# Alternating reads of the streamed operand, and one 512-column product per high part, in a hybrid decoder layer

## The chip, the cores and the metric

The kernel runs on one core of a Trainium2 chip. The metric is the time of one execution on the device in microseconds (us); of several runs the median is given. The core has a matrix engine (TensorE, in the profile PE, its weight loads PEld), a vector engine (DVE), a scalar engine (ACT), GpSimd (POOL) and SyncE (SP), which issues most of the DMAs.

## What is computed

The reference is one decoder layer for 256 positions and a model width of 2048, in float32. Cut to what matters:

```python
h = rmsnorm(x, attn_norm_w)
z, xbc, dt_raw, q, k, v, g = split(h @ w_in)          # 2048 -> 4096, 6144, 64, 3 x 2048, 4096
y_ssm  = ssd_mixer(z, xbc, dt_raw, ...) @ w_ssm_out   # 4096 -> 2048
y_attn = moba_attention(q, k, v, ...) @ w_attn_out    # 2048 -> 2048
g_ssm, g_attn = split(sigmoid(g + b_gate))
x = x + (g_ssm * y_ssm + g_attn * y_attn) @ w_out
h = rmsnorm(x, ffn_norm_w)
u_gate, u_up = split(causal_dwconv(h @ w_up, ...))    # 2048 -> 2 x 5632
x = x + (silu(u_gate) * u_up) @ w_down                # 5632 -> 2048
```

With 256 positions, attention has one block, and the SSD mixer one chunk.

## The kernel before

Nearly all the work is large products of a weight matrix with the 256 positions. A product in float32 is made of three products in a shorter float form (F32R): each operand is split into a high part (a rounded copy) and a low part (what is left), and high x high, high x low and low x high are summed.

**A unit.** The weights come in units of 128 partitions x 2048 columns, that is 16 blocks of 128 x 128: 128 output channels, all 2048 input channels. `unit` (L172) issues the unit's DMA (1 MB, on SP) into `wraw`, and splits it in two chunks of 1024 columns: ACT copies the high part `whi` (L182), DVE subtracts to get the low part `wlo` (L183). `wraw`, `whi` and `wlo` have three buffers each, so `whi` and `wlo` hold a unit and a half.

**Its products.** `cm_unit` (L220) lets `cm_chunk` (L211) run through the blocks of each chunk: for every block of the high part two matmuls of 256 columns with the same weights, one streaming the inputs' high part `xh` (L215), one the low part `xl` (L216); then for every block of the low part one matmul with `xh` (L218). The weights are the stationary operand, the 256 positions the streamed one. So a unit has 48 matmuls, all of them accumulated in 256 columns of one PSUM bank (tile `mm`, four buffers). Each matmul loads its own weights.

**Inputs.** `r32` (L240) makes tiles with both parts of an input, 2 x 16 x 256 columns: `hp` (the input with the norm's weights, for value, query, key and attention-gate units), `ot` (attention), `hn` (the normed input, for the SSD and SSD-gate units), `yt` (SSD output, 2 x 8 blocks), `mt` (the merged branches), `fh` (the second norm's input), and `a0`, `a1` (activations of the up products, in three parts of 16, 16 and 12 blocks). They share three slots.

**Order.** First the value products: here the inputs are stationary and the weights streamed, 512 columns at a time (`tm_chunk`, L370; L376, L377 and L382 are high x high, low x high and high x low). Then eight attention pairs of four query and key units each (L574), the last value block among them; attention's small work is spread over them step by step (`Spread`), and a hand-written order of PE holds in this stage. Then 16 gate units (`gate_attn`, L610) and 16 attention output units (L670); then, with the order left to the scheduler, eight SSD groups of ten units (L747) with the SSD core's steps between them, among these the product `ydot` (L834), whose streamed operand `mhl` holds a high and a low part (L840: 2 x 256 columns, L841: 2 x 128); 16 SSD gate units (L900) and 32 SSD output units (`out_unit`, L882); 16 output units (`out_products`, L966); and 88 up units (`up`, L999) and 48 down units (`down`, L1027) in thirds.

**What takes a product away.** Each unit's sum in PSUM is read by ACT or DVE: query and key units by ACT (square and scaled copy, L451 and L452), gates by DVE (L614), attention output by DVE (L672), SSD units by ACT and three DVE products (L753 to L757), output units by DVE (L976, then ACT L977 and DVE L978 write `fh`), up units by DVE (L1013, then ACT L1015 and DVE L1018 do the convolution), down units by DVE (L1038). The last down unit is added in two halves of 128 columns (L1035), each sent out by its own DMA.

Of the kernel before, what the change touches and what calls it, by code (L numbers as in the profile page):

```python
# [8 lines left out]
F32 = mybir.dt.float32  # L9
# [112 lines left out]

# [38 lines left out]
def _body(tc, nc, d, out):  # L161
# [48 lines left out]

    def cm_chunk(ps, part, xh, xl, k0, nk, first, last):  # L211
        hi, lo = part
        for k in range(nk):
            w = hi[:, k * 128:(k + 1) * 128]
            PE.matmul(ps, w, xh[:, k0 + k], start=first and k == 0, stop=False)  # L215
            PE.matmul(ps, w, xl[:, k0 + k], start=False, stop=False)  # L216
        for k in range(nk):
            PE.matmul(ps, lo[:, k * 128:(k + 1) * 128], xh[:, k0 + k], start=False, stop=last and k == nk - 1)  # L218

    def cm_unit(src, xh, xl, nk=16):  # L220
        parts = unit(src, nk * 128)
        ps = mm_tile()[:, :T]
        for c in range(2):
            cm_chunk(ps, parts[c], xh, xl, c * nk // 2, nk // 2, c == 0, c == 1)
        return ps
# [17 lines left out]

    _, hph, hpl = r32("hp")
    xt_full = xs_slot("xt")
# [124 lines left out]
    def tm_chunk(pst, part, k0, first, last):  # L370
        hi, lo = part
        for k in range(2):
            wh = hi[:, k * 512:(k + 1) * 512]
            for tt in range(2):
                ts = slice(tt * 128, (tt + 1) * 128)
                PE.matmul(pst[tt], hph[:, k0 + k, ts], wh, start=first and k == 0, stop=False)  # L376
                PE.matmul(pst[tt], hpl[:, k0 + k, ts], wh, start=False, stop=False)  # L377
        for k in range(2):
            wl = lo[:, k * 512:(k + 1) * 512]
            for tt in range(2):  # L380
                ts = slice(tt * 128, (tt + 1) * 128)
                PE.matmul(pst[tt], hph[:, k0 + k, ts], wl, start=False, stop=last and k == 1)  # L382

# [51 lines left out]

    _, oh_, ol_ = r32("ot")
    ap.tile([128, 8], F32, name="pad3")
# [6 lines left out]
    def attn_pair(j):  # L444
        st = {}

        def evac(key, h, ps):
            if h == 0:
                st["n" + key] = ap.tile([128, 2, T], F32, name="n" + key, bufs=2)
                st["s" + key] = ap.tile([128, 2, T], F32, name="sq", bufs=2)  # L450
            S.activation(st["s" + key][:, h], ps, AF.Square)  # L451
            S.activation(st["n" + key][:, h], ps, AF.Copy, scale=sm("qn") if key == "q" else kscale)  # L452

# [118 lines left out]
        for i in range(4):  # L572
            key = "qk"[i // 2]
            evac(key, i % 2, cm_unit(d["wqk"][j, i], hph, hpl))  # L574
# [55 lines left out]
    sp.tick()  # L630
    pg6 = cm_unit(d["wga"][6], hph, hpl)
    sp.flush()
# [7 lines left out]
    def hn_steps():  # L640
        xr = {}

        def load(c):
            def f():
                xr[c] = xb.tile([128, 4, T], F32, name="xr", bufs=2)
                nc.gpsimd.dma_start(xr[c], d["xT"][:, 4 * c:4 * c + 4])
            return f

        def norm(c):
            def f():  # L650
                x = xr.pop(c)
# [3 lines left out]
                S.activation(hnh[:, ks], x, AF.Copy)  # L655
                V.tensor_tensor(hnl[:, ks], x, hnh[:, ks].bitcast(F32), op=SUB)
            return f

        return [[load(0), load(1)], [], [norm(0), load(2)], [], [norm(1), load(3)], [], norm(2), [], norm(3)]

    sp.add(hn_steps(), 18)
    for o in range(KT):
# [5 lines left out]
        if o == 3:  # L668
            gl[6] = gate_attn(6, pg6)
        po = cm_unit(d["wao"][o], oh_, ol_)  # L670
        g = gl.pop(o)
        V.tensor_tensor(g, g, po, op=MUL)  # L672
        if o % 2:
# [21 lines left out]
    def dt_unit():  # L695
# [4 lines left out]
        for c in range(2):  # L700
# [4 lines left out]
            for k in range(8):  # L705
                wk = w[:, k].rearrange("p a c -> p (a c)")
                PE.matmul(ps, wk, hnh[:, 8 * c + k], start=c == 0 and k == 0, stop=False)
                PE.matmul(ps, wk, hnl[:, 8 * c + k], start=False, stop=c == 1 and k == 7)
        return ps
# [34 lines left out]
    def group_units(g):  # L744
        pr = pre[g % 2]
        for i in range(10):
            ps = cm_unit(d["wssd"][g, i], hnh, hnl)  # L747
            if i < 4:
# [11 lines left out]
    def core_steps(g):  # L760
# [73 lines left out]
        def ydot(p):  # L834
            def f():
                m = st.pop(("m", p))
                for h in range(2):
                    ps = c_tile().rearrange("p (a t) -> p a t", t=T)
                    x0, x1 = [st["x"][:, s, p, 2 * h:2 * h + 2].rearrange("p a c -> p (a c)") for s in range(2)]
                    PE.matmul(ps, x0, m[:, :, h, 0:256], start=True, stop=False)  # L840
                    PE.matmul(ps[:, :, 128:], x1, m[:, :, h, 256:384], start=False, stop=True)  # L841
                    rs, ls = slice(h * 64, (h + 1) * 64), slice(64 - h * 64, 128 - h * 64)
# [39 lines left out]
    def out_unit(q, u, done):  # L882
        parts = unit(d["wso"][q, u])
        yh, yl = yt[:, q % 2, 0], yt[:, q % 2, 1]
        ps = mm_tile()
        for c in range(2):
            cm_chunk(ps[:, c * T:(c + 1) * T], parts[c], yh, yl, 0, 8, True, True)
        done(u, ps.rearrange("p (a t) -> p a t", t=T))

    def acc_done(q):  # L890
        def f(u, ps):
            y = yacc[:, 2 * u:2 * u + 2]
            if q == 0:
# [5 lines left out]
    def gate_ssm(o):  # L899
        pg = cm_unit(d["wgs"][o], hnh, hnl)  # L900
        if o >= 8:
# [30 lines left out]

    _, mh_, ml_ = r32("mt")

    def merge(u, ps):
# [10 lines left out]
        nc.gpsimd.dma_start(a, ma[u])  # L946
        V.tensor_tensor(yacc[:, os_], ps, yacc[:, os_], op=ADD)
        V.tensor_tensor(yacc[:, os_], yacc[:, os_], g, op=MUL)
# [12 lines left out]
    for c in range(4):  # L961
        S.dma_start(x1[:, 4 * c:4 * c + 4], d["xT"][:, 4 * c:4 * c + 4])
    _, fh, fl = r32("fh")
    ssum = fp.tile([128, T], F32, name="ssum")

    def out_products():  # L966
        parts = [unit(d["wout"][o]) for o in range(2)]
        pss = [mm_tile()[:, :T] for _ in range(2)]
        for c in range(2):
            for o in range(2):  # L970
                cm_chunk(pss[o], parts[o][c], mh_, ml_, 8 * c, 8, c == 0, c == 1)
        for o in range(KT):
# [26 lines left out]
    def up(th):  # L999
# [5 lines left out]
        for i in range(n):  # L1005
            cv = []
            for half in range(2):
                ti = half * NFF + f0 + i
                ps = cm_unit(d["wup"][ti], fh, fl)
# [3 lines left out]
                V.tensor_tensor(u, ps, fr, op=MUL)  # L1013
                c = fp.tile([128, T], F32, name=f"c{half}", bufs=2)
# [12 lines left out]
    def down(th):  # L1027
        at = acts[th]
        n = thirds[th][1]
        for o in range(KT):  # L1030
            ps = cm_unit(d[wd[th]][o], at[:, 0], at[:, 1], n)
            if th == 2 and o == KT - 1:
                for h, q in enumerate((S, nc.sync)):
                    hs = slice(h * 128, (h + 1) * 128)
                    V.tensor_tensor(x1[:, o, hs], ps[:, hs], x1[:, o, hs], op=ADD)  # L1035
# [35 lines left out]
```

## Time and profile before

| | |
|---|---|
| median of 3 runs | 2019.43 us |
| lowest and highest | 2018.99, 2019.73 us |
| span of the profiled execution, first to last instruction | 2017.6 us |
| instructions in the span | 40769 |
| from HBM, to HBM | 394.44 MB, 5.33 MB |
| DMA issues of 1 MB | one per unit, landing some 4.8 us after issue |

The profiled execution's own time is known by its span alone; it lies 1.8 us under the median of the runs. The profile's lines give for a group of instructions the line of the kernel, the engine, what is written and read, the shape and the number; behind the bar the busy time in us, the mean duration of one in ns, and the idle time of the engine before them with what ended it. [...] The timeline gives start and duration of instructions in us.

### The profile page before, as it was taken

To read this page: it belongs to the slowest core of one execution; us is meant where nothing else is said; L and a number is where in the kernel's file an instruction comes from. 1 tells how busy PE (TensorE), PEld (TensorE's weight loads), DVE (VectorE), ACT (ScalarE), POOL (GpSimd) and SP (SyncE) were. 2 spreads that over 40 slices of the span, in tenths; PEclk is the share of its full clock that TensorE was granted. 3 is DMA by queue.
4 is the path that set the end of the run, shared out by engine and by line. 5 is a ranking of instruction groups with operands and counts; after the bars stand their busy time and mean duration, and the time that the engine had idled before them with its cause. 6 is when DMAs were issued, how large, how long until landed. Compare 5 with 4: busy or idle time off the path is not lost.

```text
span 2017.6 us, 40769 instructions
## 1 busy us (share of the span) xinstructions
PE 2012.3 (100%) x17203; PEld 1989.1 (99%) x17203; DVE 1496.5 (74%) x2214; ACT 1189.5 (59%) x1640; POOL 79.0 (4%) x100
## 2 busy tenths in 40 slices
PE   9999999999999999999999999999999999999999
PEld 7999999999999999999999999999999999999999
DVE  7588877656788798888989886677777765677554
ACT  6466655544768867667677645565555553455333
POOL 0012210000000000000000000000000000000000
PEclk9999999999999999999999999999999999999999
DMA  7555555656556555555565575555555555555555
GB/s 290 188 187 183 181 177 206 234 204 215 188 192 217 205 199 208 194 196 190 196 208 178 197 276 200 190 189 198 199 189 191 201 194 189 194 201 190 190 186 169
DMA packets 64351, 402.40 MB, mean 199 GB/s; under 512 B 7655, under 2 KB 10264, under 8 KB 20648
## 3 DMA queue, kind: packets, MB, share of 16 engines
q1 hardware_dynamic: 55384, 376.56, 52.9%
q0 software_dynamic: 5760, 18.97, 3.1%
q10 hardware_dynamic: 3024, 4.27, 0.6%
q8 instruction: 134, 2.20, 0.4%
q14 instruction: 49, 0.40, 0.1%
HBM read 394.44 MB, written 5.33 MB: 198 GB/s over the span
## 4 chain that ended last, share of the span: by engine, by line
PE 99%; DVE 0%; DMA 0%; issue 0%; SPq 0%; ACT 0%; DVEq 0%
PE mm L215 31%; PE mm L218 31%; PE mm L216 31%; PE mm L382 1%; PE mm L376 1%; PE mm L377 1%; PE cc L840 1%; PE cc L841 0%; PE cc L793 0%; DMA wraw<-wv 0%; PE cc L228 0%; PE cc L229 0%; PE cc L230 0%; PE cc L561 0%; DVE wlo L183 0%; DVE xt L318 0%
## 5 line engine op out<-in xcount | busy, mean ns | idle before, releaser
L182 ACT ACTIVATE whi<-wraw 128x1024 fp32r<-128x1024 f32 (+1 forms) x712 | 744.7, 1050 | 664.7 <-PE mm L216 583.2
L183 DVE TENSOR_TENSOR wlo<-wraw,whi 128x1024 fp32r<-128x1024 f32 (+1 forms) x712 | 864.1, 1218 | 242.9 <-ACT whi L182 238.0
L215 PE MATMUL mm<-hn,whi 128*128 128x256 f32 x1536 | 358.7, 277 | 0.0
L216 PE MATMUL mm<-hn,whi 128*128 128x256 f32 x1536 | 358.3, 277 | 0.0
L215 PE MATMUL mm<-fh,whi 128*128 128x256 f32 x1408 | 327.9, 277 | 0.0
L216 PE MATMUL mm<-fh,whi 128*128 128x256 f32 x1408 | 327.8, 276 | 0.0
L215 PEld LDWEIGHTS mm<-hn,whi 128*128 128x128 f32 x1536 | 288.4, 188 | 1.5 <-ACT whi L182 0.2
L216 PEld LDWEIGHTS mm<-hn,whi 128*128 128x128 f32 x1536 | 288.5, 188 | 0.1
L215 PEld LDWEIGHTS mm<-fh,whi 128*128 128x128 f32 x1408 | 264.4, 188 | 0.0
L216 PEld LDWEIGHTS mm<-fh,whi 128*128 128x128 f32 x1408 | 264.3, 188 | 0.0
L218 PE MATMUL mm<-hn,wlo 128*128 128x256 f32 x1536 | 205.6, 277 | 0.0
L218 PEld LDWEIGHTS mm<-hn,wlo 128*128 128x128 f32 x1536 | 188.4, 188 | 0.0
L218 PE MATMUL mm<-fh,wlo 128*128 128x256 f32 x1408 | 188.2, 277 | 0.0
L215 PE MATMUL mm<-hp,whi 128*128 128x256 f32 x768 | 180.1, 278 | 0.0
L216 PE MATMUL mm<-hp,whi 128*128 128x256 f32 x768 | 179.2, 277 | 0.0
L218 PEld LDWEIGHTS mm<-fh,wlo 128*128 128x128 f32 x1408 | 172.7, 188 | 0.0
L215 PE MATMUL mm<-a,whi 128*128 128x256 f32 x704 | 164.4, 277 | 0.0
L216 PE MATMUL mm<-a,whi 128*128 128x256 f32 x704 | 164.3, 276 | 0.0
L216 PEld LDWEIGHTS mm<-hp,whi 128*128 128x128 f32 x768 | 144.3, 188 | 0.1
L215 PEld LDWEIGHTS mm<-hp,whi 128*128 128x128 f32 x768 | 144.3, 188 | 0.1
L215 PEld LDWEIGHTS mm<-a,whi 128*128 128x128 f32 x704 | 132.2, 188 | 0.0
L216 PEld LDWEIGHTS mm<-a,whi 128*128 128x128 f32 x704 | 132.2, 188 | 0.0
(308 smaller groups left out, 3244.1 us busy)
## 6 DMA issues: line engine op xcount, KB each, us to landing
wraw<-wup SPq DMA_DIRECT2D x88, 1024.0 KB, 4.8
wraw<-wssd SPq DMA_DIRECT2D x80, 1024.0 KB, 4.9
wraw<-wqk SPq DMA_DIRECT2D x32, 1024.0 KB, 4.8
wraw<-wso SPq DMA_DIRECT2D x32, 1024.0 KB, 4.9
wraw<-wd SPq DMA_DIRECT2D x32, 1024.0 KB, 4.8
wraw<-wga SPq DMA_DIRECT2D x16, 1024.0 KB, 5.0
wraw<-wao SPq DMA_DIRECT2D x16, 1024.0 KB, 5.0
wraw<-wgs SPq DMA_DIRECT2D x16, 1024.0 KB, 4.8
```

What stands on the lines that cost most here:

```text
L182: last_hi[0] = S.activation(hi[:, :n // 2], raw[:, s], AF.Copy)
L183: V.tensor_tensor(lo[:, :n // 2], raw[:, s], hi[:, :n // 2].bitcast(F32), op=SUB)
L215: PE.matmul(ps, w, xh[:, k0 + k], start=first and k == 0, stop=False)
L216: PE.matmul(ps, w, xl[:, k0 + k], start=False, stop=False)
L218: PE.matmul(ps, lo[:, k * 128:(k + 1) * 128], xh[:, k0 + k], start=False, stop=last and k == nk - 1)
L376: PE.matmul(pst[tt], hph[:, k0 + k, ts], wh, start=first and k == 0, stop=False)
L377: PE.matmul(pst[tt], hpl[:, k0 + k, ts], wh, start=False, stop=False)
L382: PE.matmul(pst[tt], hph[:, k0 + k, ts], wl, start=False, stop=last and k == 1)
L840: PE.matmul(ps, x0, m[:, :, h, 0:256], start=True, stop=False)
```

## The change

Three things are changed, together.

**Reading in turn.** A streamed row of 256 columns is read as column 0, 128, 1, 129 and so on, in place of 0, 1, 2, 3: `mix` views the row as two halves and takes one column of each in turn. The result is written to PSUM without gaps, so its columns stand in that mixed order. Where the input can be stored to suit, it is: `hn`, `fh` and the host's layout of the value weights hold the even positions in the first half and the odd ones in the second, so that the products come out in natural order. Elsewhere (`hp`, `ot`, `mt`, `yt`, `a0`, `a1`) the reader of PSUM undoes it with a step of two columns (`unmix`). The value units do it with their 512 streamed columns (halves of 256), and `ydot` takes high and low part in turn.

**Wide products.** In gate, attention output, output, up and down units each block of the high part is loaded once, for one matmul of 512 columns that streams the input's high and low part; the two sums go to the two halves of the PSUM bank, and the low part's product to the first half. Query, key, SSD, SSD gate and SSD output units keep two matmuls of 256.

**Adding the two halves.** Gates, attention output and up products copy the second half with ACT and add it with DVE before the work that was there; output and down products add both halves to `x1` with DVE one after the other.

The core of the difference:

```diff
 def _tm(w, c0, n):
-    v = w[:, c0:c0 + n * 512].reshape(4, 4, 128, n, 512).transpose(3, 0, 2, 1, 4)
+    v = w[:, c0:c0 + n * 512].reshape(4, 4, 128, n, 256, 2).transpose(3, 0, 2, 1, 5, 4)
...
+def mix(x):
+    return x.rearrange("p (a b) -> p b a", a=2)
+def mixed(ps):
+    return ps.rearrange("p (b a) -> p b a", a=2)
+def unmix(ps):
+    return ps.rearrange("p (b a) -> p a b", a=2)
+def halves(x):
+    return x.rearrange("p (a b) -> p a b", a=2)
...
-            PE.matmul(ps, w, xh[:, k0 + k], start=first and k == 0, stop=False)
-            PE.matmul(ps, w, xl[:, k0 + k], start=False, stop=False)
+            start = first and k == 0
+            if wide:
+                PE.matmul(ps.rearrange("p (h b a) -> p h b a", h=2, a=2), w,
+                          x2[:, :, k0 + k].rearrange("p h (a b) -> p h b a", a=2), start=start, stop=False)
+            else:
+                PE.matmul(mixed(ps), w, mix(x2[:, 0, k0 + k]), start=start, stop=False)
+                PE.matmul(mixed(ps), w, mix(x2[:, 1, k0 + k]), start=False, stop=False)
         for k in range(nk):
-            PE.matmul(ps, lo[:, k * 128:(k + 1) * 128], xh[:, k0 + k], start=False, stop=last and k == nk - 1)
+            PE.matmul(mixed(ps[:, :T]), lo[:, k * 128:(k + 1) * 128], mix(x2[:, 0, k0 + k]), start=False,
+                      stop=last and k == nk - 1)
...
-                PE.matmul(pst[tt], hph[:, k0 + k, ts], wh, start=first and k == 0, stop=False)
+                PE.matmul(mixed(pst[tt]), hph[:, k0 + k, ts], mix(wh), start=first and k == 0, stop=False)
...
-            S.activation(st["s" + key][:, h], ps, AF.Square)
+            S.activation(halves(st["s" + key][:, h]), unmix(ps), AF.Square)
...
-        V.tensor_tensor(g, pg, rb, op=MUL)
+        S.activation(halves(g), unmix(pg[:, T:]), AF.Copy)
+        V.tensor_tensor(halves(g), unmix(pg[:, :T]), halves(g), op=ADD)
+        V.tensor_tensor(g, g, rb, op=MUL)
...
-        V.tensor_tensor(g, g, po, op=MUL)
+        t = xb.tile([128, T], F32, name="wat", bufs=2)
+        S.activation(t, po[:, T:], AF.Copy)
+        V.tensor_tensor(t, po[:, :T], t, op=ADD)
+        V.tensor_tensor(halves(g), halves(g), unmix(t), op=MUL)
...
-                    PE.matmul(ps, x0, m[:, :, h, 0:256], start=True, stop=False)
-                    PE.matmul(ps[:, :, 128:], x1, m[:, :, h, 256:384], start=False, stop=True)
+                    mt = m[:, :, h].rearrange("p a t -> p t a")
+                    PE.matmul(pt, x0, mt[:, 0:256], start=True, stop=False)
+                    PE.matmul(pt[:, 128:], x1, mt[:, 256:384], start=False, stop=True)
...
+    def add_halves(x, ps):
+        for h in (1, 0):
+            V.tensor_tensor(halves(x), unmix(ps[:, h * T:(h + 1) * T]), halves(x), op=ADD)
...
-        V.tensor_tensor(x1[:, o], ps, x1[:, o], op=ADD)
-        S.activation(fh[:, o], x1[:, o], AF.Copy, scale=sm("ffn_w", o))
+        add_halves(x1[:, o], ps)
+        S.activation(halves(fh[:, o]), unmix(x1[:, o]), AF.Copy, scale=sm("ffn_w", o))
...
-                V.tensor_tensor(u, ps, fr, op=MUL)
+                S.activation(u, ps[:, T:], AF.Copy)
+                V.tensor_tensor(u, ps[:, :T], u, op=ADD)
+                V.tensor_tensor(u, u, fr, op=MUL)
...
-            V.tensor_tensor(x1[:, o], ps, x1[:, o], op=ADD)
+            add_halves(x1[:, o], ps)
...
-                    V.tensor_tensor(x1[:, o, hs], ps[:, hs], x1[:, o, hs], op=ADD)
+                    for i in (1, 0):
+                        V.tensor_tensor(x1[:, o, hs], unmix(ps[:, i * T:(i + 1) * T])[:, h], x1[:, o, hs], op=ADD)
```

More of the change, by code (lines that the diff above doesn't have):

```diff
@@ L209, in c_tile, with cm_chunk, cm_unit @@
         return psum.tile([128, 512], F32, name="cc", bufs=4)
-    def cm_chunk(ps, part, xh, xl, k0, nk, first, last):
+    def cm_chunk(ps, part, x2, k0, nk, first, last):
         hi, lo = part
+        wide = ps.shape[-1] == 2 * T
         for k in range(nk):
             w = hi[:, k * 128:(k + 1) * 128]
-            PE.matmul(ps, w, xh[:, k0 + k], start=first and k == 0, stop=False)
-            PE.matmul(ps, w, xl[:, k0 + k], start=False, stop=False)
+            start = first and k == 0
[5 more added lines that the diff above has]
+                PE.matmul(mixed(ps), w, mix(x2[:, 1, k0 + k]), start=False, stop=False)
         for k in range(nk):
-            PE.matmul(ps, lo[:, k * 128:(k + 1) * 128], xh[:, k0 + k], start=False, stop=last and k == nk - 1)
-    def cm_unit(src, xh, xl, nk=16):
+            PE.matmul(mixed(ps[:, :T]), lo[:, k * 128:(k + 1) * 128], mix(x2[:, 0, k0 + k]), start=False,
+                      stop=last and k == nk - 1)
+    def cm_unit(src, x2, nk=16, wide=True):
         parts = unit(src, nk * 128)
-        ps = mm_tile()[:, :T]
+        ps = mm_tile()
+        if not wide:
+            ps = ps[:, :T]
         for c in range(2):
-            cm_chunk(ps, parts[c], xh, xl, c * nk // 2, nk // 2, c == 0, c == 1)
+            cm_chunk(ps, parts[c], x2, c * nk // 2, nk // 2, c == 0, c == 1)
         return ps
@@ L242, in r32 @@
         return t, t[:, 0], t[:, 1]
-    _, hph, hpl = r32("hp")
+    hp2, hph, hpl = r32("hp")
     xt_full = xs_slot("xt")
@@ L375, in tm_chunk @@
                 ts = slice(tt * 128, (tt + 1) * 128)
-                PE.matmul(pst[tt], hph[:, k0 + k, ts], wh, start=first and k == 0, stop=False)
-                PE.matmul(pst[tt], hpl[:, k0 + k, ts], wh, start=False, stop=False)
+                PE.matmul(mixed(pst[tt]), hph[:, k0 + k, ts], mix(wh), start=first and k == 0, stop=False)
+                PE.matmul(mixed(pst[tt]), hpl[:, k0 + k, ts], mix(wh), start=False, stop=False)
         for k in range(2):
@@ L381, in tm_chunk @@
                 ts = slice(tt * 128, (tt + 1) * 128)
-                PE.matmul(pst[tt], hph[:, k0 + k, ts], wl, start=False, stop=last and k == 1)
+                PE.matmul(mixed(pst[tt]), hph[:, k0 + k, ts], mix(wl), start=False, stop=last and k == 1)
     def tm_units(srcs, after_unit, before=None, mid=None):
@@ L434, in _body @@
         evac(cb, pst)
-    _, oh_, ol_ = r32("ot")
+    ot2, oh_, ol_ = r32("ot")
     ap.tile([128, 8], F32, name="pad3")
@@ L450, in evac @@
                 st["s" + key] = ap.tile([128, 2, T], F32, name="sq", bufs=2)
-            S.activation(st["s" + key][:, h], ps, AF.Square)
-            S.activation(st["n" + key][:, h], ps, AF.Copy, scale=sm("qn") if key == "q" else kscale)
+            S.activation(halves(st["s" + key][:, h]), unmix(ps), AF.Square)
+            S.activation(halves(st["n" + key][:, h]), unmix(ps), AF.Copy, scale=sm("qn") if key == "q" else kscale)
         def sums(key):
@@ L573, in attn_pair @@
             key = "qk"[i // 2]
-            evac(key, i % 2, cm_unit(d["wqk"][j, i], hph, hpl))
+            evac(key, i % 2, cm_unit(d["wqk"][j, i], hp2, wide=False))
             if i == 1:
@@ L630, in _body @@
     sp.tick()
-    pg6 = cm_unit(d["wga"][6], hph, hpl)
+    pg6 = cm_unit(d["wga"][6], hp2)
     sp.flush()
@@ L654, in f @@
                 ks = slice(4 * c, 4 * c + 4)
-                S.activation(hnh[:, ks], x, AF.Copy)
-                V.tensor_tensor(hnl[:, ks], x, hnh[:, ks].bitcast(F32), op=SUB)
+                xe_ = x.rearrange("p k (b a) -> p k a b", a=2)
+                h4, l4 = [t[:, ks].rearrange("p k (a b) -> p k a b", a=2) for t in (hnh, hnl)]
+                S.activation(h4, xe_, AF.Copy)
+                V.tensor_tensor(l4, xe_, h4.bitcast(F32), op=SUB)
             return f
@@ L706, in dt_unit @@
                 wk = w[:, k].rearrange("p a c -> p (a c)")
-                PE.matmul(ps, wk, hnh[:, 8 * c + k], start=c == 0 and k == 0, stop=False)
-                PE.matmul(ps, wk, hnl[:, 8 * c + k], start=False, stop=c == 1 and k == 7)
+                PE.matmul(mixed(ps), wk, mix(hnh[:, 8 * c + k]), start=c == 0 and k == 0, stop=False)
+                PE.matmul(mixed(ps), wk, mix(hnl[:, 8 * c + k]), start=False, stop=c == 1 and k == 7)
         return ps
@@ L746, in group_units @@
         for i in range(10):
-            ps = cm_unit(d["wssd"][g, i], hnh, hnl)
+            ps = cm_unit(d["wssd"][g, i], hnt, wide=False)
             if i < 4:
@@ L883, in out_unit @@
         parts = unit(d["wso"][q, u])
-        yh, yl = yt[:, q % 2, 0], yt[:, q % 2, 1]
         ps = mm_tile()
         for c in range(2):
-            cm_chunk(ps[:, c * T:(c + 1) * T], parts[c], yh, yl, 0, 8, True, True)
-        done(u, ps.rearrange("p (a t) -> p a t", t=T))
+            cm_chunk(ps[:, c * T:(c + 1) * T], parts[c], yt[:, q % 2], 0, 8, True, True)
+        done(u, ps.rearrange("p (o b a) -> p o a b", o=2, a=2))
     def acc_done(q):
         def f(u, ps):
-            y = yacc[:, 2 * u:2 * u + 2]
+            y = yacc[:, 2 * u:2 * u + 2].rearrange("p o (a b) -> p o a b", a=2)
             if q == 0:
@@ L899, in gate_ssm @@
     def gate_ssm(o):
-        pg = cm_unit(d["wgs"][o], hnh, hnl)
+        pg = cm_unit(d["wgs"][o], hnt, wide=False)
         if o >= 8:
@@ L930, in _body @@
             sp.add(core_steps(step), nu)
-    _, mh_, ml_ = r32("mt")
+    mt2, mh_, ml_ = r32("mt")
     def merge(u, ps):
@@ L946, in merge @@
         nc.gpsimd.dma_start(a, ma[u])
-        V.tensor_tensor(yacc[:, os_], ps, yacc[:, os_], op=ADD)
+        y4 = yacc[:, os_].rearrange("p o (a b) -> p o a b", a=2)
+        V.tensor_tensor(y4, ps, y4, op=ADD)
         V.tensor_tensor(yacc[:, os_], yacc[:, os_], g, op=MUL)
@@ L967, in out_products @@
         parts = [unit(d["wout"][o]) for o in range(2)]
-        pss = [mm_tile()[:, :T] for _ in range(2)]
+        pss = [mm_tile() for _ in range(2)]
         for c in range(2):
             for o in range(2):
-                cm_chunk(pss[o], parts[o][c], mh_, ml_, 8 * c, 8, c == 0, c == 1)
+                cm_chunk(pss[o], parts[o][c], mt2, 8 * c, 8, c == 0, c == 1)
         for o in range(KT):
-            yield o, pss[o] if o < 2 else cm_unit(d["wout"][o], mh_, ml_)
+            yield o, pss[o] if o < 2 else cm_unit(d["wout"][o], mt2)
+    def add_halves(x, ps):
+        for h in (1, 0):
+            V.tensor_tensor(halves(x), unmix(ps[:, h * T:(h + 1) * T]), halves(x), op=ADD)
     for o, ps in out_products():
-        V.tensor_tensor(x1[:, o], ps, x1[:, o], op=ADD)
-        S.activation(fh[:, o], x1[:, o], AF.Copy, scale=sm("ffn_w", o))
-        V.scalar_tensor_tensor(fl[:, o], x1[:, o], sm("ffn_w", o), fh[:, o].bitcast(F32), op0=MUL, op1=SUB)
+        add_halves(x1[:, o], ps)
+        S.activation(halves(fh[:, o]), unmix(x1[:, o]), AF.Copy, scale=sm("ffn_w", o))
+        V.scalar_tensor_tensor(halves(fl[:, o]), unmix(x1[:, o]), sm("ffn_w", o), halves(fh[:, o].bitcast(F32)),
+                               op0=MUL, op1=SUB)
         if o == 0:
```

13 lines of the change are left out of this document (7 added, 6 removed).

## Prediction

> **What bounds the kernel now.** I read the page first: the busy shares, the granted clock and the chain that ended last.
>
> ```profile
> span 2017.6 us, 40769 instructions
> PE 2012.3 (100%) x17203; PEld 1989.1 (99%) x17203; DVE 1496.5 (74%) x2214; ACT 1189.5 (59%) x1640; POOL 79.0 (4%) x100
> PEclk9999999999999999999999999999999999999999
> PE 99%; DVE 0%; DMA 0%; issue 0%; SPq 0%; ACT 0%; DVEq 0%
> PE mm L215 31%; PE mm L218 31%; PE mm L216 31%; PE mm L382 1%; PE mm L376 1%; PE mm L377 1%; PE cc L840 1%; PE cc L841 0%; PE cc L793 0%; DMA wraw<-wv 0%; PE cc L228 0%; PE cc L229 0%; PE cc L230 0%; PE cc L561 0%; DVE wlo L183 0%; DVE xt L318 0%
> ```
>
> TensorE is the chain, at full granted clock, and 93% of it are three lines: high part by high input (L215), high by low (L216), low by high (L218). A busy PE says nothing of its pace, so next come windows (us, then busy time and count for PE, weight loads, DVE, ACT, POOL, then clock, DMA share, GB/s).
>
> ```profile
> 5.00:60.00 55.00, 53.87 (x234) 42.90 (x234) 43.34 (x74) 36.93 (x61) 1.38 (x2) 1.00 0.78 284
> 730.00:1050.00 320.00, 320.00 (x2782) 318.31 (x2781) 278.81 (x410) 220.69 (x307) 8.60 (x16) 1.00 0.57 198
> 1280.00:1620.00 340.00, 340.00 (x3001) 339.96 (x3000) 252.07 (x378) 197.31 (x258) 0.00 (x0) 1.00 0.56 195
> ```
>
> In the up and first down units (1280 to 1620) 3001 matmuls take 340.0 us: one each 113.3 ns, all of 256 columns but one. The time of the kernel is this step times their number. What does it consist of? Three places in the timeline (start, duration, both in us) give steps of other shapes: value units with 512 columns, the SSD product, whose 512 columns are two pieces of 256, and transpositions, whose stream is 128 columns.
>
> ```profile
> 60.64 0.39 PE L376 MATMUL mm<-whi,hp 128*128 128x512 f32 x1
> ...
> 63.39 0.40 PE L376 MATMUL mm<-whi,hp 128*128 128x512 f32 x1
> ```
>
> ```profile
> 557.34 0.40 PE L840 MATMUL cc<-mhl,xx 128*128 128x512 f32 x1
> 557.57 0.28 PE L841 MATMUL cc<-mhl,xx 128*128 128x256 f32 x1
> 557.69 0.40 PE L840 MATMUL cc<-mhl,xx 128*128 128x512 f32 x1
> 557.93 0.28 PE L841 MATMUL cc<-mhl,xx 128*128 128x256 f32 x1
> 558.05 0.28 PE L215 MATMUL mm<-hn,whi 128*128 128x256 f32 x1
> ```
>
> ```profile
> 539.33 0.89 PEld L793 LDWEIGHTS cc<-small,slotA 128*128 128x128 f32 x8
> 539.42 1.04 PE L793 MATMUL cc<-small,slotA 128*128 128x128 f32 x8
> 540.18 0.19 PEld L228 LDWEIGHTS cc<-bch 128*128 128x128 f32 x1
> ...
> 540.29 0.19 PEld L229 LDWEIGHTS cc<-bcl,bch 128*128 128x128 f32 x1
> ```
>
> The twelve 512-column steps of a value chunk last 63.39 - 60.64 = 2.75 us, 229 ns each: more than 2 x 113.3 = 226.6. The SSD product's two pairs take 558.05 - 557.34 = 0.71 us, 0.355 for 768 columns, and its steps stand 2 to 1 (0.23 and 0.12): 237 for 512 columns and 118 for 256. So a step grows with its columns and has no fixed part that one load instead of two could save: halving the loads gains nothing by itself. But a load alone is quicker than the step: from the first transposition to the ninth load, issued as the eighth transposition starts, are seven steps in 0.76 us, 109 ns, and the load of L228, of the same type as the large units', is followed by the next after 0.11. A 256-column step is thus 3 to 4 ns longer than its load needs. What fills them is the stream: its pace differs with how the operand lies in SBUF (0.443 ns a column at 113.3, 0.447 at 229, 0.462 in the SSD product). That is what the change touches.
>
> **The change part by part.** First the count of what is touched:
>
> ```profile
> L215 PE MATMUL mm<-hn,whi 128*128 128x256 f32 x1536 | 358.7, 277 | 0.0
> L215 PE MATMUL mm<-fh,whi 128*128 128x256 f32 x1408 | 327.9, 277 | 0.0
> L215 PE MATMUL mm<-hp,whi 128*128 128x256 f32 x768 | 180.1, 278 | 0.0
> L215 PE MATMUL mm<-a,whi 128*128 128x256 f32 x704 | 164.4, 277 | 0.0
> L215 PE MATMUL mm<-yt,whi 128*128 128x256 f32 x512 | 119.4, 277 | 0.0
> L215 PE MATMUL mm<-ot,whi 128*128 128x256 f32 x256 | 59.7, 277 | 0.0
> L215 PE MATMUL mm<-mt,whi 128*128 128x256 f32 x256 | 59.6, 276 | 0.0
> L376 PE MATMUL mm<-whi,hp 128*128 128x512 f32 x128 | 50.6, 395 | 0.9 <-ACT whi L198 0.9
> L840 PE MATMUL cc<-mhl,xx 128*128 128x512 f32 x64 | 24.1, 398 | 0.0
> ```
>
> These are 5440 high parts in all. The up (fh), down (a), attention-output (ot) and output (mt) units and 256 of hp (16 gate units of 16) become wide: 1408 + 704 + 256 + 256 + 256 = 2880 pairs turn into one matmul of 512 columns. The other 2560 pairs stay pairs, and all 5440 low products stay at 256: 5120 + 5440 + 32 (the step sizes' unit) = 10592 matmuls of 256. To these come 384 of the value units (128 on each of three lines) and 64 + 64 of the SSD product. All now read columns 0, half, 1, half + 1 and so on. PE's order in an up unit, before:
>
> ```order
> L215 MATMUL mm<-fh,whi 128x256
> L216 MATMUL mm<-fh,whi 128x256
> L215 MATMUL mm<-fh,whi 128x256
> L216 MATMUL mm<-fh,whi 128x256
> L218 MATMUL mm<-fh,wlo 128x256 x8
> ```
>
> and in the changed kernel, a whole unit:
>
> ```order
> L234 MATMUL mm<-fh,whi 128x512 x8
> L240 MATMUL mm<-fh,wlo 128x256 x8
> L234 MATMUL mm<-fh,whi 128x512 x8
> L240 MATMUL mm<-fh,wlo 128x256 x8
> ```
>
> Nothing moves past anything; 16 short steps of a chunk become 8 long ones, and the columns stay the same.
>
> No row has a stream that alternates, so its pace is bounded. From below by the loads: a 256-column step cannot be under its load, 109 (the transpositions); I take 110, the load of L228. For 512 columns the low end is twice the mean of the eight loads from 539.33 to 540.18, 2 x 106 = 212.5, since nothing in the trace passes 128 columns faster; the other end is 2 x 110 = 220; I take the middle, 216. From above there is no bound (the rivals). I take the gain because the three paces above show that the layout of what is streamed sets the pace, while the 113.3 are the same in stages with DVE 74% and 87% busy (340.0/3001 = 113.3 against 320/2782 = 115.0 with the longer SSD products in it), so that it is not the other engines' traffic.
>
> [...]
>
> The sum, by rows: wide pairs 2880 x (226.6 - 216) = 30.5 us. Steps of 256: 10592 x (113.3 - 110) = 35.0. Value units 384 x (229 - 216) = 5.0. SSD 64 x (237 - 216) + 64 x (118 - 110) = 1.9. Together 72.4 us, all on PE, which is the chain.
>
> The price is on ACT and DVE. A wide unit has its two partial products in two halves of a bank, so they must be added: in gates, attention output and up products one ACT copy and one DVE add each, in output and down products a second DVE add. Rows of such operations, and of the splitting that PE needs:
>
> ```profile
> L182 ACT ACTIVATE whi<-wraw 128x1024 fp32r<-128x1024 f32 (+1 forms) x712 | 744.7, 1050 | 664.7 <-PE mm L216 583.2 <-PE mm L377 23.2 <-issue 20.6
> L1013 DVE TENSOR_TENSOR u<-mm,fr 128x256 f32<-128x256 f32 x88 | 37.3, 425 | 93.8 <-PE mm L218 93.7
> L846 DVE TENSOR_TENSOR slotA<-cc,slotA 64x256 f32<-64x256 f32 x64 | 27.0, 422 | 2.0
> ```
>
> DVE in the up products, before:
>
> ```order
> L1013 TENSOR_TENSOR u<-mm,fr_15874 128x256
> L183 TENSOR_TENSOR wlo<-wraw,whi 128x1024
> L1018 SCALAR_TENSOR_TENSOR c_17957<-u,small,c_17957 128x255
> L1018 SCALAR_TENSOR_TENSOR c_17957<-u,small,c_17957 128x254
> L183 TENSOR_TENSOR wlo<-wraw,whi 128x1024
> ```
>
> and changed (L1053 is the add of the halves, L1054 the old product with the norm, L199 the split):
>
> ```order
> L1053 TENSOR_TENSOR u<-mm,u 128x256
> L1054 TENSOR_TENSOR u<-u,fr_15202 128x256
> L199 TENSOR_TENSOR wlo<-wraw,whi 128x1024
> L1059 SCALAR_TENSOR_TENSOR c_16851<-u,small,c_16851 128x255
> L1059 SCALAR_TENSOR_TENSOR c_16851<-u,small,c_16851 128x254
> L199 TENSOR_TENSOR wlo<-wraw,whi 128x1024
> ```
>
> DVE gets 0.42 us a unit, and before it waits for ACT's copy of the product's second half, which waits for the unit's last matmul. Queued behind each are the splits of later weights (L198, L199), for which PE waits. The cover: ACT's split today already waits for PE to free a buffer (583.2 us), and three buffers of half a unit mean that a split stands a unit ahead, some 5 us; a copy of about 0.4 in front uses little of that. DVE waits 93.8 us in 88 units for PE, about 1.07 a unit, and is 252 of 340 us busy; with 62 units of 0.42 more in a PE time some 4% shorter it is 278 of 328, 85%. So I cost it at nothing; were the cover gone, it would be 0.42 us in each of the 168 + 16 wide units, 77 us, the whole gain. The strided PSUM reads (query, key, SSD) add no instruction. [...] I take nothing, as no work is added. The weights' DMAs are the same; 1 MB in 5.2 us is about 200 GB/s, and the start of the kernel moved 284. The low parts of ot, mt and fh are now read with the high ones and so some steps earlier; they were written well ahead.
>
> One place is bare, the end:
>
> ```profile
> 2013.83 0.62 PE L218 MATMUL mm<-a,wlo 128*128 128x256 f32 x4
> 2014.48 0.49 DVE L1035 TENSOR_TENSOR x<-mm,x 128x128 f32<-128x128 f32 x2 [3.65 <-PE mm L218]
> ```
>
> Two adds follow the last matmul, about 0.29 each; four will: +0.6 us.
>
> Sum -72.4 + 0.6 = -71.8. The span of 2017.6 lies 1.8 us under the runs' median of 2019.4; what lies around it stays: 2019.4 - 71.8 = 1948.
>
> **The rivals.** *Only long streams gain.* The 113.3 could be a load that is slower under a running stream (the 0.11 of L228 had none beside it). Then 256-column steps stay: 30.5 + 5.0 + 1.3 - 0.6 = 36 us, 1983. For it: seven different inputs all have the same duration, 276 to 278. Against: the SSD product's steps stand 2 to 1 by columns, with the same loads under them.
>
> *The pace is not a matter of read order.* Then 256 stays, and a wide step takes 226.6, 2020; or, since it has two pieces of 256 like L840, 237: 2880 x 10.4 = 30 us, 2050. It decides from 226.6 up. For it: L840 is the only such form here. Against: the change reads just that product the other way as well.
>
> *Each jump costs a beat.* Today's streams run along a row; the new ones leave it at each column. If that takes two beats, the streams of 10592 x 113.3 + 2880 x 226.6 + 384 x 229 and the SSD's, 1.96 ms, double: about 3980. It is slower as soon as a column costs over 0.443 ns. The trace shows no jump, for or against. [...]
>
> **How the numbers follow.** The runs lie within 0.04%, so 0.2%, 4 us, is what a measurement can tell. Forecast 0.50, long streams only 0.26, read order irrelevant 0.09 (0.05 within 4 us, 0.04 slower), jumps cost 0.12, and 0.03 for a gain partly given back to DVE. Faster 0.50 + 0.26 + 0.03 = 0.79, same 0.05, slower 0.16. Low end: 109 and 212.5: 45.5 + 40.6 + 6.3 + 2.1 - 0.6 = 94, 1926. High end: the unchanged pace, 2020, which leaves out the jumps and the 2050, 0.16.
>
> **What would show it.** Right: steps of 110 for 256 and 216 for 512 in the up window, PE without idle time, DVE at 85% there, four adds at the end. Wrong: 512 columns at 226 or more; or 113 still in the SSD stage's units; or PE waiting for L199.

## The result and the profile after

The changed kernel takes 1965.43 us (median of 4 runs, 1965.15 to 1967.04) against 2019.58 us: a ratio of 0.973, with a 95% interval of 0.972 to 0.975. The forecast was 1948. Of the page, the span, PE's busy time and the chain:

```profile
span 1963.6 us, 35306 instructions
PE 1955.8 (100%) x14323; PEld 1861.7 (95%) x14323; DVE 1567.6 (80%) x2399; ACT 1207.6 (62%) x1758; POOL 78.6 (4%) x100
PE 97%; DVE 2%; ACT 0%; issue 0%; DMA 0%; DVEq 0%; ACTq 0%
PE mm L234 32%; PE mm L240 30%; PE mm L237 14%; PE mm L238 14%; PE mm L407 1%; PE mm L401 1%; PE mm L402 1%; DVE wlo L199 1%; PE cc L874 1%; PE cc L825 0%; PE cc L875 0%; DVE slotA L788 0%; DMA xw<-x 0%; PE cc L253 0%; PE cc L255 0%
```

PE is still the chain, with 2880 instructions fewer, and loads are now 95% of the span in place of 99%: a long step has room beside its one load. The steps are read from the timeline, from start to start, since the records overlap: one of 256 columns lasts 0.28 us, and the next starts 0.11 us after it. First the up units (L234 is the wide product, L240 the low part's), then an SSD unit (L237, L238), then a value unit:

```profile
1299.65 1.67 PE L234 MATMUL mm<-fh,whi 128*128 128x512 f32 x7
1301.16 1.05 PE L240 MATMUL mm<-fh,wlo 128*128 128x256 f32 x8
1302.05 0.38 PE L234 MATMUL mm<-fh,whi 128*128 128x512 f32 x1
```

```profile
800.11 0.28 PE L237 MATMUL mm<-hn,whi 128*128 128x256 f32 x1
...
801.45 0.28 PE L240 MATMUL mm<-hn,wlo 128*128 128x256 f32 x1
```

```profile
60.27 0.38 PE L401 MATMUL mm<-whi,hp 128*128 128x512 f32 x1
...
62.85 0.38 PE L401 MATMUL mm<-whi,hp 128*128 128x512 f32 x1
```

Seven wide steps take 1301.16 - 1299.65 = 1.51 us, 216 ns each. Twelve steps of an SSD unit take 1.34, 111.7 each (before: 113.3). Eight low products take 0.89, 111. Twelve value steps take 2.58, 215 each (before: 229). Over the whole trace, start to start, the 2880 wide steps have a mean of 216.4, the steps of 256 columns 111.7 (before 113.5), the SSD product's 218 and 109 (before 236 and 118).

The vector engine, in the windows of the SSD and up stages (PE, PEld, DVE, ACT, POOL busy, clock, DMA share, GB/s), PE's largest wait, and the end:

```profile
712.00:1027.00 315.00, 315.00 (x2786) 313.79 (x2785) 279.53 (x413) 219.98 (x307) 8.60 (x16) 1.00 0.59 201
1243.00:1570.00 327.00, 326.93 (x1997) 299.97 (x1997) 275.25 (x436) 205.96 (x314) 0.00 (x0) 1.00 0.57 201
```

```profile
663.10 0.38 PE L237 MATMUL mm<-hn,whi 128*128 128x256 f32 x1 [1.58 <-ACT whi L198]
```

```profile
1959.87 1.14 DVE L1077 TENSOR_TENSOR x<-mm,x 128x128 f32<-128x128 f32 x4 [3.05 <-PE mm L240]
```

DVE is busy 89% and 84% of these stages and PE 315.0 and 326.9 us of them: the adds, which are new in the second, are hidden. One new wait of 1.6 us stands in the SSD stage, where ACT's split is late. The four adds at the end are there.

### The profile page after: what moved, and what is told of

It reads as the page before. It is cut to its first block, busy times and chain, and to the rows that moved or that the text cites. A ratio compares the mean times of both kernels' runs of the same rounds, so it can differ in the third digit from the quotient of the medians.

```text
span 1963.6 us, 35306 instructions
## 1 busy us (share of the span) xinstructions
PE 1955.8 (100%) x14323; PEld 1861.7 (95%) x14323; DVE 1567.6 (80%) x2399; ACT 1207.6 (62%) x1758; POOL 78.6 (4%) x100
## 4 chain that ended last, share of the span: by engine, by line
PE 97%; DVE 2%; ACT 0%; issue 0%; DMA 0%; DVEq 0%; ACTq 0%
PE mm L234 32%; PE mm L240 30%; PE mm L237 14%; PE mm L238 14%; PE mm L407 1%; PE mm L401 1%; PE mm L402 1%; DVE wlo L199 1%; PE cc L874 1%; PE cc L825 0%; PE cc L875 0%; DVE slotA L788 0%; DMA xw<-x 0%; PE cc L253 0%; PE cc L255 0%
## 5 line engine op out<-in xcount | busy, mean ns | idle before, releaser
L199 DVE TENSOR_TENSOR wlo<-wraw,whi 128x1024 fp32r<-128x1024 f32 (+1 forms) x712 | 863.8, 1219 | 257.5 <-ACT whi L198 248.8
L237 PE MATMUL mm<-hn,whi 128*128 128x256 f32 x1536 | 353.3, 275 | 1.7 <-ACT whi L198 1.6
L238 PE MATMUL mm<-hn,whi 128*128 128x256 f32 x1536 | 353.0, 275 | 0.0
L234 PE MATMUL mm<-fh,whi 128*128 128x512 f32 x1408 | 333.4, 380 | 0.1
L237 PEld LDWEIGHTS mm<-hn,whi 128*128 128x128 f32 x1536 | 294.9, 192 | 2.7 <-ACT whi L198 2.0
L238 PEld LDWEIGHTS mm<-hn,whi 128*128 128x128 f32 x1536 | 295.0, 192 | 0.1
L234 PEld LDWEIGHTS mm<-fh,whi 128*128 128x128 f32 x1408 | 253.3, 190 | 28.6 <-DVE fh L1016 0.5
L240 PE MATMUL mm<-hn,wlo 128*128 128x256 f32 x1536 | 202.9, 275 | 0.0
L240 PEld LDWEIGHTS mm<-fh,wlo 128*128 128x128 f32 x1408 | 184.6, 191 | 9.4
L240 PEld LDWEIGHTS mm<-hn,wlo 128*128 128x128 f32 x1536 | 186.9, 192 | 0.0
L240 PE MATMUL mm<-fh,wlo 128*128 128x256 f32 x1408 | 185.6, 275 | 0.0
L234 PE MATMUL mm<-a,whi 128*128 128x512 f32 x704 | 167.8, 380 | 0.0
L234 PEld LDWEIGHTS mm<-a,whi 128*128 128x128 f32 x704 | 126.0, 190 | 13.7
L237 PE MATMUL mm<-hp,whi 128*128 128x256 f32 x512 | 118.2, 276 | 0.0
L237 PE MATMUL mm<-yt,whi 128*128 128x256 f32 x512 | 117.7, 275 | 0.0
L238 PE MATMUL mm<-hp,whi 128*128 128x256 f32 x512 | 117.7, 275 | 0.0
L238 PE MATMUL mm<-yt,whi 128*128 128x256 f32 x512 | 117.6, 275 | 0.0
L240 PE MATMUL mm<-hp,wlo 128*128 128x256 f32 x768 | 101.4, 275 | 0.0
L238 PEld LDWEIGHTS mm<-yt,whi 128*128 128x128 f32 x512 | 98.3, 192 | 0.3
L237 PEld LDWEIGHTS mm<-yt,whi 128*128 128x128 f32 x512 | 98.3, 192 | 0.3 <-ACT whi L198 0.2
L240 PEld LDWEIGHTS mm<-a,wlo 128*128 128x128 f32 x704 | 93.5, 191 | 5.1
```

Of the source, the lines that this page charges most:

```text
L199: V.tensor_tensor(lo[:, :n // 2], raw[:, s], hi[:, :n // 2].bitcast(F32), op=SUB)
L234: PE.matmul(ps.rearrange("p (h b a) -> p h b a", h=2, a=2), w, x2[:, :, k0 + k].rearrange("p h (a b) -> p h b a", a=2), start=start, stop= ...
L237: PE.matmul(mixed(ps), w, mix(x2[:, 0, k0 + k]), start=start, stop=False)
L238: PE.matmul(mixed(ps), w, mix(x2[:, 1, k0 + k]), start=False, stop=False)
L240: PE.matmul(mixed(ps[:, :T]), lo[:, k * 128:(k + 1) * 128], mix(x2[:, 0, k0 + k]), start=False, stop=last and k == nk - 1)
```

## The experiments

The theory: the order in which a streamed operand is read sets its pace; 512 columns read in turn from two halves pass in 216 ns, and a step of 256 columns is then bounded by its weight load. Rivals: the loads saved are the gain; or reading in turn helps only where one load serves 512 columns; and for the short step, that its stream or the issue of an instruction pair bounds it, not the load.

**Wide products, read in plain order.** `mix` and its companions return their argument as it is, inputs are stored in natural order, and `ydot` reads as before the change:

```diff
 def mix(x):
-    return x.rearrange("p (a b) -> p b a", a=2)
+    return x
...
-                PE.matmul(ps.rearrange("p (h b a) -> p h b a", h=2, a=2), w,
-                          x2[:, :, k0 + k].rearrange("p h (a b) -> p h b a", a=2), start=start, stop=False)
+                PE.matmul(ps.rearrange("p (h b) -> p h b", h=2), w, x2[:, :, k0 + k], start=start, stop=False)
```

> Wide products as in the changed kernel, but every stream is read in plain order. Read order theory: a contiguous stream of 512 columns in two pieces takes 229 to 237 ns as the value units and the SSD product did, and steps of 256 columns stay at 113.3 ns; 2880 wide steps cost 2.4 to 10.4 ns more than two short ones, so 2027 to 2050 us, slower than before. Rival, that the loads saved are the gain: wide steps at 216 ns in any order, 2880 x 10.6 = 30 us gained, about 1990 us.

2040.23 us (2038.85 to 2041.22); ratio to before 1.010, 1.009 to 1.012. Its timeline in the up units:

```profile
1399.70 1.33 PE L234 MATMUL mm<-fh,whi 128*128 128x512 f32 x5
1400.87 1.07 PE L239 MATMUL mm<-fh,wlo 128*128 128x256 f32 x8
1401.78 2.02 PE L234 MATMUL mm<-fh,whi 128*128 128x512 f32 x8
```

Five wide steps take 1.17 us, 233 each, between the 229 and 237 of before; the low ones 0.91 / 8 = 114. Half the loads with the same columns are a loss: the rival falls.

**Reading in turn, no wide products.** `cm_unit` has `wide=False` everywhere, and gates, attention output, up, output and down sums are taken away as before the change:

```diff
-    def cm_unit(src, x2, nk=16, wide=True):
+    def cm_unit(src, x2, nk=16, wide=False):
...
-                S.activation(u, ps[:, T:], AF.Copy)
-                V.tensor_tensor(u, ps[:, :T], u, op=ADD)
-                V.tensor_tensor(u, u, fr, op=MUL)
+                V.tensor_tensor(u, ps, fr, op=MUL)
```

> Alternating reads as in the changed kernel, but no wide products: all units keep two matmuls of 256 columns per high part, and the sums are taken away as before the change. Read order theory: all 16352 steps of 256 columns at 111.7 ns as in the changed kernel's SSD units, 1.6 ns each or 26 us, and 7 us in value units and SSD product: about 1987 us. Rival, that reading in turn helps only where one load serves 512 columns: steps of 113.3 ns, and only the 7 us, about 2013 us.

1987.28 us (1986.17 to 1988.36); ratio 0.984, 0.983 to 0.986. The up stage in a window:

```profile
1260.00:1590.00 330.00, 330.00 (x2956) 329.95 (x2956) 246.79 (x370) 193.99 (x253) 0.00 (x0) 1.00 0.56 196
```

330.0 / 2956 = 111.6 ns a step. So reading in turn gives 32 us alone, wide products cost 21 alone, and both together gave 53 beside them (1966.44, the changed kernel of the next paragraph): wide products are worth 21 us only with the reading in turn.

**The changed kernel again,** unchanged, beside these and once more beside the last version below.

> The changed kernel again, beside the others on the same chip. All theories: 1965 us within 2 us.

> The changed kernel again beside that. All theories: 1966 us within 2 us.

1966.44 us (1965.27 to 1968.23) and 1965.30 (1965.14 to 1966.90).

**A shorter stream, the same load.** Two kernels leave the low product out for 32 positions: the changed one and the one before.

```diff
-            PE.matmul(mixed(ps[:, :T]), lo[:, k * 128:(k + 1) * 128], mix(x2[:, 0, k0 + k]), start=False,
-                      stop=last and k == nk - 1)
+            PE.matmul(mixed(ps[:, :T])[:, :112], lo[:, k * 128:(k + 1) * 128], mix(x2[:, 0, k0 + k])[:, :112],
+                      start=False, stop=last and k == nk - 1)
```

> The changed kernel, but each low part's product streams 224 of the 256 positions (the low part's contribution to 32 positions is left out). If a step of 256 columns is bounded by its load: low steps stay at 111.7 ns, and the time at 1965 us. If by its stream: 7/8 of that, 98 ns, 5440 x 13.9 = 76 us less, about 1890 us.

> The kernel before, with each low part's product streaming 224 of the 256 positions, in plain order (the low part's contribution to 32 positions is left out). Read order theory: today's 113.3 ns are the stream's and lie a little above the load's; so the step falls only to the load's 109 to 112 ns: 7 to 23 us less, 1996 to 2012 us. Rival, that 113.3 ns are the load under a running stream: no change, 2019 us. Third, that no load bounds it: 99 ns, 1943 us.

The steps, in the changed kernel's variant and in that of before:

```profile
1302.35 1.04 PE L240 MATMUL mm<-fh,wlo 128*128 128x224 f32 x8
1303.23 0.61 PE L234 MATMUL mm<-fh,whi 128*128 128x512 f32 x2
```

```profile
1401.81 1.05 PE L218 MATMUL mm<-fh,wlo 128*128 128x224 f32 x8
1402.69 0.28 PE L215 MATMUL mm<-fh,whi 128*128 128x256 f32 x1
```

Eight low products take 0.88 us in both, 110 each. Within them, the first (96 and 100 ns) goes by its stream; in the changed kernel's variant the rest stand at 112 each, as with 256 columns, and in that of before at 108 to 116, 113 in the mean. What the first one gains comes back behind the row: the next wide step takes 232 ns in place of 218, and in the variant of before the next four steps take 122 to 114. So a chunk without waits takes as long with the shorter stream as with the whole one, in the median 2620 ns in the changed kernel (eight wide steps and eight low ones) and 2720 in the kernel before (24 steps). The up units of the variant of before, in a window:

```profile
1330.00:1670.00 340.00, 339.95 (x3000) 339.75 (x2999) 254.13 (x382) 196.78 (x256) 0.00 (x0) 1.00 0.55 195
```

That is 3000 matmuls in 340 us, where the kernel before has 3001 in the same time, though here a third of them stream an eighth less. So a short step does not follow its stream, neither after the change, where it stays at 112, nor before it, where it stays at 113. This is the second expectation's rival, the load under a running stream, and not the 109 to 112 of the read order theory. That it is the load is shown for the changed kernel by the next experiment; the kernel before was not run with a shorter load.

The times answered neither theory: 2009.05 and 2047.17 us in one run each, 28 to 43 us more than the kernels they come from, with less work. There PE waits for the splits, 95 and 49 steps of over 260 ns against 29 and 20, and behind some of these waits its clock is lower for a while (granted clock 0.997 and 0.998 over the two executions). Counted from the first matmul of each stage, the changed kernel's variant loses 15 us in the attention output units, 18 from the first SSD unit to the first output unit, and 10 in the up and down units; that of before loses 12, 15 and less than 1. The first line of the waits of PE's loads in the changed kernel's variant (us in total, times, longest):

```profile
PEld mm L240 <- DVE wlo L199: 40.2, 50, 3.8
```

With shorter products the scheduler has put DVE's work in another order. In the attention output units products of a norm (L680), whose input comes by DMA, stand in a row ahead of the split (L199) that PE waits for:

```profile
332.81 1.67 DVE L680 SCALAR_TENSOR_TENSOR xr<-xr,small,rb 128x256 f32<-128x256 f32 x4 [3.79 <-DMA xr<-xT]
336.24 1.28 DVE L680 SCALAR_TENSOR_TENSOR xr<-xr,small,rb 128x256 f32<-128x256 f32 x3 [1.76 <-DMA xr<-xT]
337.43 1.22 DVE L685 TENSOR_TENSOR hn<-xr,hn 128x1024 fp32r<-128x1024 f32 x1
338.56 1.22 DVE L199 TENSOR_TENSOR wlo<-wraw,whi 128x1024 fp32r<-128x1024 f32 x1
```

```profile
339.84 1.15 PE L240 MATMUL mm<-ot,wlo 128*128 128x224 f32 x8 [2.97 <-DVE wlo L199]
```

The changed kernel has a split between these products. In the up units the variant has the convolution (L1059) ahead of the next split, where the changed kernel has the split first:

```
L1053 TENSOR_TENSOR u<-mm,u 128x256
L1054 TENSOR_TENSOR u<-u,fr_15202 128x256
L1059 SCALAR_TENSOR_TENSOR c_16902<-u,small,c_16902 128x255
L1059 SCALAR_TENSOR_TENSOR c_16902<-u,small,c_16902 128x254
L1063 TENSOR_TENSOR c_16851<-c_16851,c_16902 128x256
L199 TENSOR_TENSOR wlo<-wraw,whi 128x1024
```

That the order costs the time is argued from these waits; no run changes the order alone.

**A shorter load, the same stream.** The low part's weights are 96 of 128 columns in all but a unit's last product.

```diff
+            end = last and k == nk - 1
+            m = 128 if end else 96
+            PE.matmul(mixed(ps[:m, :T]), lo[:, k * 128:k * 128 + m], mix(x2[:, 0, k0 + k]), start=False, stop=end)
```

> The changed kernel, but each low part's weights are 96 of 128 columns in all but the last low product of a unit (the low part's contribution to 32 output channels is left out). If the load of 128 columns bounds the step at 111.7 ns, it now falls to the stream's pace, half of a wide step, 108 to 109 ns: 5440 x 3.2 = 17 us less, about 1948 us. If what bounds it is one instruction pair's issue, whatever the size: 111.7 ns and 1965 us.

1959.57 us in one run. The row of eight such products and the one that follows:

```profile
1302.03 1.04 PE L242 MATMUL mm<-fh,wlo 128*96 128x256 f32 x8
1302.91 0.38 PE L234 MATMUL mm<-fh,whi 128*128 128x512 f32 x1
```

0.88 / 8 = 110 ns, the median over the trace 109: with a shorter load the step falls to the stream's pace. So in the changed kernel it is the load, not the issue of a pair. The time falls by 6 us and not by 17. A chunk falls from 2620 to 2605 ns (eight wide steps and eight low ones) or from 2680 to 2662 (24 steps), which makes 11 us, since the step falls by less than the 3.2 ns reckoned and the first low step behind a wide one was at 109 already. Longer waits for the splits, and the lower clock behind one of them (below), take the rest.

**Read orders.** The value units stream 512 columns with one load each, 229 ns a step before and 216 in the changed kernel, where a short step bounded by its load takes 112: no load hides the stream's pace. In three kernels each of the four blocks of value columns reads in an order of its own, 96 steps each.

```diff
+ORDERS = [('p a -> p a', {}), ('p (b a) -> p a b', {'a': 2}), ('p (a b) -> p b a', {'a': 4}), ('p (c a b) -> p c b a', {'a': 2, 'b': 4})]
...
+        turn, kw = ORDERS[cb]
...
+            return x.rearrange(turn, **kw) if kw else x
```

> The changed kernel with other read orders of the value units' 512 streamed columns, one for each of the four blocks (their value columns come out in another order). Block 0: plain order, 0 1 2 3. Block 1: even columns, then odd ones. Block 2: four quarters in turn. Block 3: columns 4 apart in turn, 0 4 1 5 2 6 3 7. Distance theory (two far places in turn are what helps): 229, 229, 216, 229 ns for a step. [...]

> The changed kernel with four more read orders of the value units' streamed columns (their value columns come out in another order). Block 0: pairs from the two halves in turn, 0 1 256 257 2 3. Block 1: columns 16 apart in turn. Block 2: fours from the two halves in turn, 0 1 2 3 256 257 258 259. Block 3: every fourth column, 0 4 8, then 1 5 9. [...] Theory that neighbours must not follow each other at once, whatever else: 229 to 273, 216, about 229, 216. [...]

> The changed kernel with read orders of the value units' 512 streamed columns once more (their value columns come out in another order). Block 0: two columns apart in turn, 0 2 1 3 4 6 5 7. Block 1: eighths in turn. Block 2: 64 apart in turn. Block 3: plain order, at another place than in the first such run. [...] If it is enough that neighbours do not follow each other: 216, slower than or like 273, 216, 229.

Medians of the 96 steps, start to start:

| order of the 512 columns | ns a step |
|---|---|
| plain, 0 1 2 3 (two places) | 229.5 and 229 |
| two halves in turn, the changed kernel | 216 |
| 64 apart in turn | 216 |
| 16 apart in turn | 216 |
| 4 apart in turn, 0 4 1 5 | 216 |
| 2 apart in turn, 0 2 1 3 | 233 |
| fours from the halves in turn | 253.5 |
| four quarters in turn | 273 |
| pairs from the halves in turn | 340 |
| even columns, then odd | 453 |
| every fourth column | 460 |
| eight eighths in turn | 487 |

Four of these in the timeline: evens, then odds, from the first kernel, 64 apart from the third, and pairs, then every fourth column, from the second.

```profile
69.08 0.64 PE L423 MATMUL mm<-whi,hp 128*128 128x512 f32 x1
69.54 0.64 PE L424 MATMUL mm<-whi,hp 128*128 128x512 f32 x1
```

```profile
81.14 0.38 PE L424 MATMUL mm<-whi,hp 128*128 128x512 f32 x1
81.36 0.38 PE L423 MATMUL mm<-whi,hp 128*128 128x512 f32 x1
```

```profile
20.09 0.51 PE L424 MATMUL mm<-whi,hp 128*128 128x512 f32 x1
20.43 0.51 PE L423 MATMUL mm<-whi,hp 128*128 128x512 f32 x1
...
241.76 0.66 PE L423 MATMUL mm<-whi,hp 128*128 128x512 f32 x1
242.22 0.66 PE L424 MATMUL mm<-whi,hp 128*128 128x512 f32 x1
```

The columns, the loads and the products are the same in all: the read order alone moves the step from 216 to 487. Distance is not it (4 columns apart do as well as 256, both at 216), and that neighbours do not follow each other is not enough (0 2 1 3 takes 233, the quarters 273). What is shown: two runs, each read neighbour after neighbour, 4, 16, 64 or 256 columns apart, one column of each in turn, take 216 ns, and 2 columns apart 233. By what mechanism the order sets the pace is not shown.

**More wide units.** The first four units of each SSD group are made wide, in one version with the 16 SSD gates, in the other alone:

```diff
-            ps = cm_unit(d["wssd"][g, i], hnt, wide=False)
+            ps = cm_unit(d["wssd"][g, i], hnt, wide=i < 4)
             if i < 4:
-                S.activation(pr[:, i], ps, AF.Copy)
+                S.activation(pr[:, i], ps[:, T:], AF.Copy)
+                V.tensor_tensor(pr[:, i], ps[:, :T], pr[:, i], op=ADD)
```

> The changed kernel with 48 more wide units: the first four of each SSD group's ten, and the 16 SSD gates, each with one ACT copy or activation and one DVE add more. If PE stays the chain: 48 x 16 x (223.4 - 216.3) = 5.5 us less than the changed kernel, about 1960 us. If DVE, 89% busy in that stage, becomes the bound: no gain or a loss, 1965 us and above, with PE waiting for the splits of the weights.

> The changed kernel with the first four units of each SSD group's ten wide, 32 in all, each with one DVE add more; the SSD gates stay as they are, since in the kernel with both wide PE waits up to 2 us there. 32 x 16 x (223.4 - 216.3) = 3.6 us less than the changed kernel, about 1962 us, if DVE hides its 32 adds; 1966 us if not.

With the gates 1964.01 us (1963.45 to 1965.25) beside 1966.44 of the changed kernel, 2.4 us less and not the 5.5 reckoned: PE waits 1.8 and 1.5 us for splits, at 612 and 694 us. The sums of the gates before them are taken away from 578 to 597 and from 660 to 678 us, so these waits stand in the wide SSD units behind the gates, and not at the gates, where the second expectation puts them. Without the wide gates 1962.78 (1962.43 to 1963.28) beside 1965.30 (1965.14 to 1966.90), ratio to before 0.972 (0.970 to 0.973): 2.5 of the 3.6 us. It is the quickest version here that computes the whole layer; its runs and the changed kernel's do not overlap, though the two intervals against before do.

## Why the prediction was right, and where a term was not

**The bound.** Right: PE is the chain before and after, and the gain is the sum of its steps.

**Loads.** Right that a saved load is worth nothing by itself; the kernel with wide products alone is 21 us slower.

**The step of 512.** Right: 216.4 was measured, and 2880 x (2 x 113.5 - 216.4) = 30.5 us, as forecast. That it came out so closely is luck: 216 was the middle of two ends that were both taken from loads, and the wide step, with one load of some 112 ns under it, goes by its stream. The rival that the pace has nothing to do with read order is refuted by the table of orders; its 237 for a wide step in plain order was near (233).

**The step of 256.** This is the term that was mis-sized, and its reading was wrong. The prediction took it that a load needs 109 to 110 ns and that the stream fills the 3 to 4 ns above, 10592 x 3.3 = 35.0 us. Measured are 111.7: 10592 x (113.5 - 111.7) = 19 us. The floor was too low: 110 came from a load that had no long stream beside it, and among loads and running streams a step keeps 112 with a shorter stream and falls to 109 only with a shorter load. And what stood above it was not the stream: in the kernel before, too, the chunk keeps its 2720 ns when an eighth of the low products' stream is left out. The rival of long streams only had put the 113.3 to the load, and this run bears it out; its conclusion, that steps of 256 columns then stay, is refuted by the kernel with reading in turn alone (111.6). So the 19 us are the read order's, but not by the way that the prediction gave. Why a short step that does not follow its stream is 1.7 ns quicker beside streams read in turn is not shown by any run here. The stream's own pace, read in turn, is 109: the first short step after a wide one takes that, and with the shorter load they all do.

**Value units and SSD product.** 384 x 13 = 5.0 us and 1.7 us, as forecast (5.0 and 1.9).

**Copies and adds.** Forecast at nothing, with DVE 85% busy in the up stage: 275 of 327 us, 84%, and the sum below closes without a term for them. What can fail is the cover of the splits, and it goes by DVE's order: in the variants with 224 columns PE waits for splits, and they take 43 and 28 us more than the kernels they come from. The 28 us are lost in a kernel that has none of the new adds, so this is not the price that the prediction named (77 us if each add were bare). One wait was not forecast, 1.6 us in the SSD stage.

**The end.** +0.6 us forecast; from the last matmul's start to the span's end it is 4.03 us after 3.39.

**The sum.** 30.5 + 19 + 5.0 + 1.7 - 0.6 - 1.6 = 54 us; the spans differ by 54.0. Against the forecast of 71.8, 16 of the missing 18 are the step of 256.

**Jumps.** The rival that each jump costs is refuted for the order of the change, which shares the lowest step, 216, and not refuted as such: every fourth column takes 460, twice as long.

## What to carry to other kernels

When a matrix engine is busy all the time, read its pace from start to start and compare it with what the same columns take in other places of the trace; a few per cent between forms of the same size (229 and 237 ns for 512 columns here) are a lead that busy time does not show. A floor for a step must come from a row in which the same things run beside it: the load taken from between transpositions was 2 ns too short, and 2 ns in ten thousand steps were the miss. Whether a step goes by its stream is found by shortening the stream, over a whole chunk, since what one step gains another can give back (here the first low step fell to 96 ns, and the next wide one rose from 218 to 232). And where an engine feeds the bound, look at what stands in its queue ahead of that work: the adds cost nothing here, while two kernels with less work, in which other work came first, took 28 and 43 us more.

## What was not expected of the hardware

The pace of a stream depends on its read order by up to a factor of 2.3 (216 to 487 ns for the same 512 columns), and plain order is not the fastest.

Some waits of PE of about 2 us are followed by a slower clock, and some are not. In the variant with 96 weight columns PE waits 2.1 us, starts again at full pace, and for some 3.4 us from 665 us on has steps of 0.21 us for 256 columns; the granted clock in the window there is 0.62 (third column from the right):

```profile
663.48 0.38 PE L237 MATMUL mm<-hn,whi 128*128 128x256 f32 x1 [2.12 <-ACT whi L198]
```

```profile
655.00:660.00 5.00, 5.00 (x48) 1.00 0.34 102
664.00:668.00 4.00, 4.00 (x25) 0.62 0.31 43
```

The kernel with the wide gates has the same after its wait of 1.8 us, and the changed kernel's variant with 224 columns does not have it after one of 2.3 us:

```profile
613.40:616.80 3.40, 3.40 (x10) 0.51 0.48 111
```

```profile
492.51 1.15 PE L240 MATMUL mm<-hn,wlo 128*128 128x224 f32 x8 [2.31 <-DVE wlo L199]
```

```profile
492.00:496.00 4.00, 3.49 (x31) 1.00 0.68 209
496.00:500.00 4.00, 4.00 (x38) 1.00 0.85 264
```

The wait of 1.6 us that the changed kernel has at the first of these places has no such sequel either. So the length of the wait alone does not decide it.
